# Up projection of an encoder layer: from the last row of the output projection on, the instructions of all five engines in a written order, with one split or sum of the next pair behind each chain

## Chip, cores, metric

One Trainium2 chip, one of its cores. The time is the device time of one execution in microseconds; of several runs the median is given. The engines of the core work in parallel, each through a queue of its own, and wait for each other by semaphores: TensorE (PE, matrix products; PEld is its weight load), VectorE (DVE), ScalarE (ACT), GpSimd (POOL) and SyncE (SP, which here issues transfers). PSUM is the memory of 8 banks into which TensorE writes; a bank holds 128 x 512 numbers in float32.

## What is computed

One layer of an encoder on 1024 tokens of width 1024: an input projection, attention in a window and a gated recurrence, a merge with an output projection, and a feed-forward part. The change concerns the seam between the last two.

```python
h = h + mix @ w_o[l]                       # output projection, residual
m = rms_norm(h, norm_mlp[l])               # a row's scale, times a gain
h = h + jnp.square(jax.nn.relu(m @ w_up[l])) @ w_down[l]
```

All inputs are float32. `w_up` is 1024 x 4096, `w_down` 4096 x 1024. The 1024 tokens are 8 row blocks of 128.

## The kernel before

**Products of float32.** An operand is split into a high part, rounded to the matmul type fp32r, and the rest: ScalarE casts (`wh`, `hi`), VectorE subtracts (`wl`, `lo`). A product is three matmuls, high by high, high by low, low by high.

**Output projection.** `wo_rows` (L889) makes half a row block by 24 matmuls and adds it into `hres` (L897). `norm_row` (L912) then issues the store of the row block, squares it on ScalarE (L919), takes 1/sqrt of the mean on GpSimd, and scales the row on VectorE (L921).

**Up projection.** It is one step of the Strassen-Winograd scheme, with seven products in place of eight. The left factor is a pair of column blocks of `w_up` (2 x 128 columns by two halves of the 1024 rows: a11, a12, a21, a22), the right one the normalised rows, transposed, in four quarters (b11, b12, b21, b22: half of the width by half of the tokens). There are NP = 16 pairs. For each, VectorE makes four sums of weights (`winograd`, L681 to L685):

```python
s1 = a21 + a22;  s2 = s1 - a11;  s3 = a11 - a21;  s4 = a12 - s2
```

and once for all pairs the rows give t1 to t4 (row loop, L948 to L951). The products are P1 = a11 b11, P2 = a12 b21, P3 = s4 b22, P4 = a22 t4, P5 = s1 t1, P6 = s2 t2, P7 = s3 t3, and each is a `chain` (L687) of 12 matmuls of 128 x 512: 4 steps of 128 rows, three matmuls each. Three banks take the seven: `pa` P1, then P1 + P2 (the block u11); `pb` P6, then P6 + P7, then P6 + P7 + P4; `pc` P3, then P3 + P5. ScalarE copies P1 and P3 out as `p1` and `p3` before the next chain goes into the same bank. VectorE and GpSimd then form the other blocks: u1 = pb + p1 + pc behind P5, u3 = pb + p1 - p3 + pc behind P7, u2 = pb + p1 behind P4. ScalarE applies ReLU and square (`relu2`, L982), and GpSimd forms four differences `S` of the blocks, which the down projection needs. All of them are stored to DRAM (`usp`), from where the down projection, which is also split like this, takes its operands.

**Weights.** `weights` (L974) splits one of a pair's seven left factors: a cast on ScalarE (L978) and a subtraction on VectorE (L979), 128 x 512 each. A pair's 1 MB of `w_up` comes by one transfer (`load_pair`, L1021), into one of two buffers. The weights' tiles `wh` and `wl` come from two pools in turn, four of each to a pool.

**Warm-up.** For the first three pairs (EARLY, L966) P1 and P2 are computed ahead (`first_products`, L989), as b11 and b21 are ready before t1 to t4 are. `to_variant` (L923) makes a piece of a right factor: TensorE transposes four 128 x 128 blocks into a bank `pt`, ScalarE casts them out (L929), VectorE subtracts (L930). Twenty such pieces remain after the last row; `psum_pools` gives this stretch the banks pa=2, a=4 (the transposes') and two for rows.

**What sets the order.** Up to here nothing is written by hand: a list scheduler decides, for each engine, in which order the instructions of this text stand, so chains, transposes and casts may be cut into each other. Only the down projection behind it has a written order (a block `manual_schedule`, L1289, in which each engine's queue keeps the order of the text).

**Main loop (L1045 to L1093).** In the text a pair's steps are: the load of the next pair, the four sums, all splits, P1 with the copy of p1, then P4 of the pair before with u2 and the last difference (`last_product`, L1035, held back by one pair), P3 with the copy of p3 (L1067), P2, P6 with u1's first sum (L1075), P5 with its second (L1077), P7, u3's three steps (L1080 on VectorE, L1081 on GpSimd, L1082 on VectorE), and the differences (L1087 to L1089). In the last pair VectorE takes the differences over from GpSimd. Behind the loop stand the operands of the down projection's first step (L1098 on) and its matmuls (`bk0`, L1115), which the casts in `split2` (L1152) follow.

Of the kernel before, what the change touches and what calls it, by code (L numbers as in the profile page):

```python
# [18 lines left out]
P = 128  # L19
# [29 lines left out]
def layer(ctx: ExitStack, tc: tile.TileContext, x, meta, w_in, w_na, w_hg, w_o, w_up, w_dn,  # L49
# [862 lines left out]
    def norm_row(i):  # L912
# [7 lines left out]
        rsqrt_mean(rs, ssq, D, tm)  # L920
        dve.scalar_tensor_tensor(hres[i], hres[i], rs, g2, op0=ALU.mult, op1=ALU.mult)  # L921

# [9 lines left out]
    for i in range(4):  # L932
        for hc in range(2):
            wo_rows(i, hc)
        norm_row(i)
    nT0 = u_tiles(0, "nT")
    nV = {"b11": [t[:, :4, :TH] for t in nT0], "b21": [t[:, 4:, :TH] for t in nT0]}

    nB = []
    for j in range(4):  # L940
        for hc in range(2):
            wo_rows(j + 4, hc)
        to_variant("a", hres[j][:, :TH], nV["b11"], j)
        to_variant("a", hres[j][:, TH:], nV["b21"], j)
        norm_row(j + 4)
        b11, b21, b12, b22 = (hres[i][:, q:q + TH] for i in (j, j + 4) for q in (0, TH))
        t2 = rowp.tile([P, TH], F32, tag="t2", name="t2", bufs=3)
        dve.tensor_tensor(b11, b12, b11, op=ALU.subtract)  # L948
        dve.tensor_tensor(t2, b22, b11, op=ALU.subtract)
        pool.tensor_tensor(b12, b22, b12, op=ALU.subtract)  # L950
        pool.tensor_tensor(b21, b21, t2, op=ALU.subtract)  # L951
        nB.append({"t1": b11, "b22": b22, "t3": b12, "t2": t2, "t4": b21})
# [33 lines left out]
    def first_tiles():  # L986
        return a_tile(upa, "p1", bufs=EARLY), a_tile(upa, "u11", bufs=EARLY)

    def first_products(w11, w12, between=lambda: None, tiles=None):  # L989
        p1, u11 = tiles or first_tiles()  # L990
        pa = up_bank("pa")
        chain(pa, w11, nV["b11"], True)
        act.copy(p1, pa)
        between()
        chain(pa, w12, nV["b21"], False)
        relu2(u11, pa)
        return p1, u11

    first_of, first_w = {}, {}

    def first_weights(m):
        raw = a_tile(upw, "sx", bufs=2, n=D).rearrange("p (k c) -> p k c", c=P)
        sp.dma_start(raw, w_up[:, 2 * m * P:(2 * m + 1) * P].rearrange("(k p) c -> p k c", p=P))
        first_w[m] = weights(raw[:, :4]), weights(raw[:, 4:])

    tiles = first_tiles()
    first_weights(0)

    for j in range(4):
        for v in nB[j]:  # L1010
            to_variant("a", nB[j][v], nV[v], j)
    rows_.close()
    hress.close()

    rawp = ups.enter_context(tc.tile_pool(name="rawp", bufs=1, side="right", reuse_waits="tile"))
    raws = {}

    def raw_tile():
        return rawp.tile([P, KC, 2 * P], F32, tag="raw", name="raw", bufs=2)

    def load_pair(m):  # L1021
        raws[m] = raw_tile()
        sp.dma_start(raws[m], w_up[:, 2 * m * P:(2 * m + 2) * P].rearrange("(k p) c -> p k c", p=P))

    load_pair(0)
    for m in range(EARLY):
        if m + 1 < EARLY:
            first_weights(m + 1)
        first_of[m] = first_products(*first_w[m], tiles=tiles if m == 0 else None)
        act.dma_start(usp[0][m][:, 0], first_of[m][1])  # L1030
    psum_pools(pa=2, pb=2, pc=2)
    upb = ups.enter_context(tc.tile_pool(name="upb", bufs=1, reuse_waits="tile"))
    w_pools.append(upb)

    def last_product(m, W, pb, p1, U, S):  # L1035
        chain(pb, W["a22"], nV["t4"], False)
        dve.tensor_tensor(U[2], pb, p1, op=ALU.add)
        relu2(U[2], U[2])
        last = m == NP - 1

# [5 lines left out]
    for m in range(NP):  # L1046
        if m + 1 < NP:
            load_pair(m + 1)
# [334 lines left out]
```

## Time and profile before

| | |
|---|---|
| median of 3 runs | 1548.38 us (1547.61 to 1549.24) |
| profiled execution, its own time | 1550.67 us |
| its span, first to last instruction | 1548.9 us |
| mean granted TensorE clock | 0.994 |
| PE busy, 0 to 860 us | 827.24 us |
| PE busy, 860 to 1245 us (last rows, up projection) | 380.75 of 385.00 us |
| PE busy, 1245 to 1549 us (down projection) | 295.16 of 304.00 us |

The views that the prediction quotes are these. The *page* gives the busy time of each engine. *Windows* are a table by stretch: start and end, length, busy time of each engine with its number of instructions, the granted clock, the share of DMA and its rate. *Waits* name the engine and line that waited, what released it, and the total, the number and the longest of these waits in us. *Timeline* rows have the start in us, the duration, engine, line, operation, output and inputs, shape, and in brackets the idle time ahead of the row and what ended it. Matmuls overlap, so their durations are longer than the distance from one to the next. `L691` to `L693` are the three matmuls of a chain's step, `L927` a group of four transposes.

### The profile page before, as it was taken

What the parts mean: (1) busy time and instruction counts of PE and PEld (TensorE: products, weight loads), DVE (VectorE), ACT (ScalarE), POOL (GpSimd) and SP (SyncE); (2) the same over time, 40 slices, a digit from 0 to 9 for tenths busy, and PEclk for the clock granted to TensorE, in tenths of its full rate; (3) what the DMA queues carried; (4) which work ended last, traced back from release to release, by engine and by line L of the source; (5) the groups of instructions that cost most, each with busy time, mean ns of one, the idle gap of its engine ahead of it and who ended that gap; (6) DMA issues with size and microseconds to landing.
All of it is one profiled execution on the core that took longest, in us unless ns stands there. A gap on an engine that the chain in (4) does not pass through costs nothing.

```text
span 1548.9 us, 23474 instructions
## 1 busy us (share of the span) xinstructions
PE 1503.1 (97%) x9188; PEld 1254.2 (81%) x9188; DVE 1010.7 (65%) x1588; ACT 657.7 (42%) x1172; POOL 407.2 (26%) x367
## 2 busy tenths in 40 slices
PE   5999999999999998999999999999999999999998
PEld 5788888887888887888888887888888788887886
DVE  6666666664976877666476368666666444879676
ACT  6231313124666666434123144555555433433444
POOL 4313121215224300011000122444444200237142
PEclk9999999999999999999999999999999999999999
DMA  5101011113123128434746124444444576563224
GB/s 181 43 28 56 28 56 29 55 29 120 57 72 119 55 68 271 137 123 151 260 161 229 55 83 140 149 157 152 155 151 144 170 273 235 190 231 105 100 82 150
DMA packets 142335, 195.61 MB, mean 126 GB/s; under 512 B 8064, under 2 KB 90112, under 8 KB 142224
## 3 DMA queue, kind: packets, MB, share of 16 engines
q1 hardware_dynamic: 133424, 172.61, 33.6%
q10 hardware_dynamic: 6624, 14.16, 2.4%
q0 software_dynamic: 2176, 7.34, 1.3%
q8 instruction: 72, 1.18, 0.3%
q14 instruction: 39, 0.32, 0.1%
HBM read 139.55 MB, written 54.53 MB: 125 GB/s over the span
## 4 chain that ended last, share of the span: by engine, by line
PE 85%; DVE 7%; issue 3%; ACT 2%; DMA 1%; POOL 1%; SPq 0%; POOLq 0%; ACTq 0%; DVEq 0%
PE mm L135 11%; PE mm L136 11%; PE mm L137 10%; PE mm L1106 4%; PE pa L1106 4%; PE pb L691 4%; PE pb L693 4%; PE pb L692 4%; PE pc L1106 4%; PE pb L1106 4%; PE pc L691 3%; PE pc L692 3%; PE pc L693 3%; PE pa L691 2%; PE pa L693 2%
## 5 line engine op out<-in xcount | busy, mean ns | idle before, releaser
L135 PE MATMUL mm<-aT,hi 128*128 128x512 f32 (+2 forms) x640 | 229.5, 359 | 2.1 <-DVE QX L563 1.5
L137 PE MATMUL mm<-aT,lo 128*128 128x512 f32 (+2 forms) x640 | 227.4, 355 | 0.0
L136 PE MATMUL mm<-aT,hi 128*128 128x512 f32 (+2 forms) x640 | 226.2, 353 | 0.0
L135 PEld LDWEIGHTS mm<-aT,hi 128*128 128x128 f32 x640 | 121.5, 190 | 16.4 <-issue 1.7
L97 DVE TENSOR_TENSOR dl<-ur,dh 128x1024 fp32r<-128x1024 f32 x55 | 76.8, 1396 | 88.4 <-ACT dh L96 88.3
L137 PEld LDWEIGHTS mm<-aT,lo 128*128 128x128 f32 x640 | 121.4, 190 | 13.2
L136 PEld LDWEIGHTS mm<-aT,hi 128*128 128x128 f32 x640 | 121.5, 190 | 12.5
L96 ACT CAST dh<-ur 128x1024 fp32r<-128x1024 f32 x55 | 57.9, 1053 | 161.3 <-issue 78.1
L125 ACT CAST hi<-raw 128x1024 fp32r<-128x1024 f32 x36 | 37.8, 1050 | 106.3 <-PE mm L136 75.5
L979 DVE TENSOR_TENSOR wl<-sx,wh 128x512 fp32r<-128x512 f32 x70 | 49.7, 719 | 32.3 <-ACT wh L978 32.3
L978 ACT CAST wh<-sx 128x512 fp32r<-128x512 f32 x70 | 42.7, 619 | 62.2 <-PE pc L692 27.3
L979 DVE TENSOR_TENSOR wl<-raw,wh 128x512 fp32r<-128x512 f32 x46 | 50.2, 1092 | 23.7 <-ACT wh L978 22.9
L1087 POOL TENSOR_TENSOR us<-u,uv 128x512 f32<-128x512 f32 x15 | 24.1, 1603 | 143.9 <-ACT uv L984 143.9
L1195 POOL TENSOR_TENSOR w<-w,tt 128x512 f32<-128x512 f32 x16 | 23.3, 1457 | 134.0 <-DVE tt L1194 106.0
L983 ACT ACTIVATE uv<-uv 128x512 f32<-128x512 f32 x48 | 30.4, 633 | 66.2 <-DVE uv L1082 49.9
L399 POOL TENSOR_TENSOR Y<-X,TN 128x512 f32<-128x512 f32 x20 | 33.8, 1690 | 88.2 <-DVE X L396 88.2
L126 DVE TENSOR_TENSOR lo<-raw,hi 128x1024 fp32r<-128x1024 f32 x34 | 45.5, 1338 | 16.1 <-ACT hi L125 15.3
L618 DVE CUSTOM_DVE_ANT_0 pr<-nsc,NB 128x432 f32<-128x432 f32 (+1 forms) x64 | 35.1, 558 | 27.0 <-PE nsc L613 26.8
L691 PE MATMUL pb<-nt,wh 128*128 128x512 f32 x128 | 51.0, 398 | 1.8 <-DVE uv L1075 1.8
L1106 PE MATMUL mm<-dl,dh 128*128 128x512 f32 x126 | 49.9, 396 | 2.1 <-DVE dl L97 2.1
L92 POOL TENSOR_SCALAR rtm<-ssq 128x1 f32<-128x1 f32 (+1 forms) x17 | 6.5, 385 | 172.2 <-ACT junk L919 157.6
L693 PE MATMUL pa<-nT,wl 128*128 128x512 f32 x128 | 50.3, 393 | 0.7 <-DVE wl L979 0.7
(381 smaller groups left out, 4422.5 us busy)
## 6 DMA issues: line engine op xcount, KB each, us to landing
raw<-in_w_in SPq DMA_DIRECT2D x56, 512.0 KB, 3.9
ur<-usp SPq DMA_DIRECT2D x55, 512.0 KB, 3.5
raw<-in_w_up SPq DMA_DIRECT2D x16, 1024.0 KB, 5.4
usp<-us SPq DMA_DIRECT2D x60, 256.0 KB, 2.0
sg<-gsp SPq DMA_DIRECT2D x16, 512.0 KB, 3.5
w<-in_w_dn SPq DMA_DIRECT2D x16, 512.0 KB, 4.5
usp<-uv SPq DMA_DIRECT2D x30, 256.0 KB, 2.3
gsp<-gv ACTq DMA_DIRECT2D x24, 256.0 KB, 2.7
```

The costliest lines, as they stand in the source:

```text
L96: act.copy(hi, src)
L97: dve.tensor_tensor(lo, src, hi.bitcast(F32), op=ALU.subtract)
L126: eng.tensor_tensor(lo[:, :kc], raw[:, :kc], hi[:, :kc].bitcast(F32), op=ALU.subtract)
L135: pe.matmul(ps, lh, rh, start=first, stop=False)
L136: pe.matmul(ps, lh, rl, start=False, stop=False)
L137: pe.matmul(ps, ll, rh, start=False, stop=last)
L691: pe.matmul(ps, lhs[0][:, c], rhs[0][:, k], start=first and k == 0, stop=False, skip_group_check=True)
L692: pe.matmul(ps, lhs[0][:, c], rhs[1][:, k], start=False, stop=False, skip_group_check=True)
L693: pe.matmul(ps, lhs[1][:, c], rhs[0][:, k], start=False, stop=k == 3, skip_group_check=True)
L978: act.copy(v(hi), src)
L979: dve.tensor_tensor(v(lo), src, v(hi).bitcast(F32), op=ALU.subtract)
L1106: pe.matmul(ps, a[n == 2][:, q, j * P:(j + 1) * P], b[n == 1][:, q], start=first and n == 0, stop=last and n == 2, skip_group_check=True)
```

## The change

The list scheduler is set aside from the last row block (row 7) of the output projection to the last product of the up projection. This stretch now stands in a `manual_schedule` block over all five engines: each engine carries out its instructions in the order of the text. To write that order, the steps are cut into functions, `product_1` to `product_7` named by product, and the main loop calls them so that behind each chain one split of the *next* pair's weights follows (`next_weights`); the four sums of the next pair (`pair_sums`) stand between u3 and P4 of the pair before. A pair's weights are loaded two pairs ahead.

```diff
+    def row_scale(i):
...
         act.dma_start(hsp[i], hres[i])
         act.activation(junk, hres[i], AF.Square, accum_out=ssq)
         rsqrt_mean(rs, ssq, D, tm)
+        return rs
+    def scale_row(i, rs):
         dve.scalar_tensor_tensor(hres[i], hres[i], rs, g2, op0=ALU.mult, op1=ALU.mult)
+    def row_sums(j):
...
+    for i in range(4, 8):
         for hc in range(2):
+            wo_rows(i, hc)
+        if i < 6:
+            for j in (2 * i - 8, 2 * i - 7):
+                to_variant("a", hres[j][:, :TH], nV["b11"], j)
+                to_variant("a", hres[j][:, TH:], nV["b21"], j)
+        if i < 7:
+            scale_row(i, row_scale(i))
+            if i > 4:
+                nB += [row_sums(j) for j in range(len(nB), i - 3)]
...
+    def next_weights(m, *vs):
+        if m + 1 == NP:
+            n = len(step0)
+            if n < 4:
+                step0.append(weights(step0_raw[0][:, n * TH:(n + 1) * TH]))
+            return
+        q = pairs[m + 1]
+        for v in vs:
+            if not (q.early and v in ("a11", "a12")):
+                q.W[v] = weights(q.A[v])
+    def product_1(q, w):
...
+        chain(q.pa, w, nV["b11"], True)
+        act.copy(q.p1, q.pa)
+    def product_2(q, w):
+        chain(q.pa, w, nV["b21"], False)
+        relu2(q.u11, q.pa)
+        (act if q.early or q.last else sp).dma_start(usp[0][q.m][:, 0], q.u11)
+    def product_3(q):
+        q.pc, q.p3 = up_bank("pc"), a_tile(upb, "p3")
+        chain(q.pc, q.W["s4"], nV["b22"], True)
+        act.copy(q.p3, q.pc)
+    def product_6(q):
...
+        chain(q.pb, q.W["s2"], nV["t2"], True)
+        dve.tensor_tensor(q.u1, q.pb, q.p1, op=ALU.add)
+    def product_5(q):
+        chain(q.pc, q.W["s1"], nV["t1"], False)
+        dve.tensor_tensor(q.u1, q.u1, q.pc, op=ALU.add)
+        relu2(q.u1, q.u1)
+    def block_out(q, v, a, b, op, dst):
+        q.S[v] = a_tile(upb, "us", bufs=4)
+        (dve if q.last else pool).tensor_tensor(q.S[v], a, b, op=op)
+        (pool if q.last else sp).dma_start(dst, q.S[v])
+    def product_7(q):
+        q.u3 = a_tile(upb, "uv", bufs=6)
+        chain(q.pb, q.W["s3"], nV["t3"], False)
+        dve.tensor_tensor(q.u3, q.pb, q.p1, op=ALU.add)
+        pool.tensor_tensor(q.u3, q.u3, q.p3, op=ALU.subtract)
+        block_out(q, 2, q.u11, q.u1, ALU.subtract, usp[2][q.m][:, 1])
+    def finish_u3(q):
+        dve.tensor_tensor(q.u3, q.u3, q.pc, op=ALU.add)
+        relu2(q.u3, q.u3)
+        (act if q.last else sp).dma_start(usp[2][q.m][:, 0], q.u3)
+        block_out(q, 0, q.u1, q.u3, ALU.add, usp[1][q.m][:, 1])
+        block_out(q, 1, q.S[0], q.u11, ALU.subtract, usp[1][q.m][:, 0])
+    def product_4(q):
...
+        chain(q.pb, q.W["a22"], nV["t4"], False)
+        dve.tensor_tensor(u2, q.pb, q.p1, op=ALU.add)
+        relu2(u2, u2)
...
+    first_load(0)
+    first_load(1)
+    first_weights(0)
+    first_weights(1)
+    first_load(2)
+    with tc.manual_schedule(engines={e.engine for e in (pe, act, dve, pool, sp)}):
+        rs7 = row_scale(7)
...
+        product_1(pairs[0], first_w[0][0])
+        transposes(0, 4)
+        scale_row(7, rs7)
+        product_2(pairs[0], first_w[0][1])
+        transposes(4, 6)
+        nB.append(row_sums(3))
+        transposes(6, 9)
+        product_1(pairs[1], first_w[1][0])
+        first_weights(2)
+        transposes(9, 14)
+        product_2(pairs[1], first_w[1][1])
+        transposes(14, 20)
...
+        load_pair(0)
+        load_pair(1)
+        product_1(pairs[2], first_w[2][0])
+        pair_sums(pairs[0])
+        next_weights(-1, "s4", "s2")
+        product_2(pairs[2], first_w[2][1])
+        psum_pools(pa=2, pb=2, pc=2)
...
+        next_weights(-1, "s1", "s3", "a22")
+        for m, q in enumerate(pairs):
+            if m + 2 <= NP:
+                load_pair(m + 2)
+            if not q.early:
+                product_1(q, q.W["a11"])
+            if m:
+                finish_u3(pairs[m - 1])
+            if m + 1 < NP:
+                pair_sums(pairs[m + 1])
+            if m:
+                product_4(pairs[m - 1])
+            next_weights(m, "a11", "s4")
+            product_3(q)
+            next_weights(m, "a12")
+            if not q.early:
+                product_2(q, q.W["a12"])
+            next_weights(m, "s2")
+            product_6(q)
+            next_weights(m, "s1")
+            product_5(q)
+            next_weights(m, "s3")
+            product_7(q)
+            next_weights(m, "a22")
+        finish_u3(pairs[-1])
+        product_4(pairs[-1])
```

`transposes(n0, n1)` calls `to_variant` for the pieces n0 to n1 - 1 of the twenty, five to a row block: t1, b22, t3, t2, t4. The seventeenth `load_pair` fetches the operands of the down projection's first step. In the rows below, numbers behind a name tell buffers apart.

ScalarE's queue at the passage from the warm-up to the loop. `pa` is the bank of pair 2's P1 and P2, the `sx` tiles hold two sums each (before, 9454 holds s1 and s2 of pair 0, 9455 s3 and s4, 9557 and 9558 those of pair 1; after, 9427, 9428 and 9485 in the same way), `pc` is the bank of pair 0's P3. Before:

```order
L978 CAST wh_9464<-sx_9454 128x512
L993 COPY p1_9407<-pa_9409 128x512
L978 CAST wh_9460<-sx_9455 128x512
L978 CAST wh_9468<-sx_9454 128x512
L978 CAST wh_9472<-sx_9455 128x512
L978 CAST wh_9476<-raw_9325 128x512
L983 ACTIVATE u11_9408<-pa_9409 128x512
L984 ACTIVATE u11_9408<-u11_9408 128x512
L1030 DMA usp0_2_8515<-u11_9408 128x512
L978 CAST wh_9567<-sx_9557 128x512
L978 CAST wh_9575<-sx_9558 128x512
L1067 COPY p3_9482<-pc_9481 128x512
```

After, the same place:

```order
L1051 COPY p1_9411<-pa_9413 128x512
L988 CAST wh_9433<-sx_9428 128x512
L988 CAST wh_9437<-sx_9427 128x512
L993 ACTIVATE u11_9412<-pa_9413 128x512
L994 ACTIVATE u11_9412<-u11_9412 128x512
L1056 DMA usp0_2_8515<-u11_9412 128x512
L988 CAST wh_9470<-sx_9427 128x512
L988 CAST wh_9474<-sx_9428 128x512
L988 CAST wh_9478<-raw_9407 128x512
L988 CAST wh_9490<-sx_9485 128x512
L1061 COPY p3_9495<-pc_9494 128x512
```

Three casts of pair 0 (s1, s3, a22) now stand behind ReLU, square and store of pair 2's u11 instead of ahead of them, and the cast ahead of the copy of p3 is now that of pair 1's s4 (wh_9490), the last of its four sums; before, those of its s2 and s3 stood there.

TensorE at the end of pair 0's P7 (`pb` its bank, nt30 and nt31 the parts of t3, nt40 and nt41 those of t4, nT10 and nT11 those of b22). Before, with `pc_9584` the bank of pair 1's P3:

```order
L691 MATMUL pb_9480<-nt30_9153,wh_9472 128x512
L692 MATMUL pb_9480<-nt31_9154,wh_9472 128x512
L693 MATMUL pb_9480<-nt30_9153,wl_9473 128x512
L691 MATMUL pc_9584<-nT10_9146,wh_9563 128x512
L692 MATMUL pc_9584<-nT11_9147,wh_9563 128x512
L693 MATMUL pc_9584<-nT10_9146,wl_9564 128x512
L691 MATMUL pc_9584<-nT10_9146,wh_9563 128x512
L691 MATMUL pb_9480<-nt40_9155,wh_9476 128x512
```

After:

```order
L691 MATMUL pb_9513<-nt30_9139,wh_9474 128x512
L692 MATMUL pb_9513<-nt31_9140,wh_9474 128x512
L693 MATMUL pb_9513<-nt30_9139,wl_9475 128x512
L691 MATMUL pb_9513<-nt40_9141,wh_9478 128x512
L692 MATMUL pb_9513<-nt41_9142,wh_9478 128x512
L693 MATMUL pb_9513<-nt40_9141,wl_9479 128x512
```

The four matmuls of pair 1's P3 that stood between P7 and P4 are gone from there: P4 follows P7 at once in the same bank.

TensorE where the second group of transposes begins (`pa` is pair 0's bank, `pt` the bank of a transpose). Before, seven pieces stand ahead of these rows, and more are cut into the chain of P2:

```order
L693 MATMUL pa_9337<-nT00_8818,wl_9177 128x512
L691 MATMUL pa_9337<-nT00_8818,wh_9176 128x512
L927 MATMUL pt_9229<-ident_80,hres5_8496 128x128 x4
L692 MATMUL pa_9337<-nT01_8819,wh_9176 128x512
L927 MATMUL pt_9236<-ident_80,t2_8975 128x128 x4
L693 MATMUL pa_9337<-nT00_8818,wl_9177 128x512
L927 MATMUL pt_9243<-ident_80,hres1_8495 128x128 x4
L927 MATMUL pt_9250<-ident_80,hres2_8489 128x128 x4
```

After, behind the whole chain of P2 and ahead of the next pair's P1:

```order
L693 MATMUL pa_9188<-nT00_8818,wl_9163 128x512
L940 MATMUL pt_9246<-ident_80,hres0_8493 128x128 x4
L940 MATMUL pt_9253<-ident_80,hres1_8495 128x128 x4
L940 MATMUL pt_9265<-ident_80,hres5_8496 128x128 x4
L940 MATMUL pt_9272<-ident_80,hres5_8496 128x128 x4
L940 MATMUL pt_9279<-ident_80,t2_9003 128x128 x4
L691 MATMUL pa_9288<-nT00_8818,wh_9166 128x512
```

Five pieces now stand in a row, for four banks; before, at most two stood together here, with matmuls of a chain around them.

157 lines of the change are left out of this document (47 added, 110 removed).

## Prediction

> **What bounds the kernel now.** I read the page first, then the busy time by stretch, then TensorE's waits in the part that the change rewrites (875 to 1245 us).
>
> ```profile
> span 1548.9 us, 23474 instructions
> PE 1503.1 (97%) x9188; PEld 1254.2 (81%) x9188; DVE 1010.7 (65%) x1588; ACT 657.7 (42%) x1172; POOL 407.2 (26%) x367
> ```
> ```profile
> core 0: us, PE busy (x) PEld busy (x) DVE busy (x) ACT busy (x) POOL busy (x), PEclk, DMA share, GB/s
> 911.00:931.00 20.00, 19.06 (x125) 15.85 (x124) 17.63 (x27) 15.69 (x30) 3.33 (x4) 1.00 0.43 146
> 961.00:969.00 8.00, 6.15 (x20) 4.36 (x19) 5.07 (x9) 2.50 (x4) 1.60 (x2) 0.79 0.57 194
> 1000.00:1200.00 200.00, 200.00 (x885) 165.58 (x884) 126.39 (x169) 104.65 (x181) 82.72 (x55) 1.00 0.44 153
> ```
> ```profile
> PE pb L691 <- DVE uv L1075: 1.8, 1, 1.8
> PE mm L1106 <- ACT dh L96: 0.7, 1, 0.7
> PE pa L693 <- DVE wl L979: 0.7, 1, 0.7
> PE mm L1106 <- DVE dl L97: 0.4, 1, 0.4
> PE pb L691 <- ACT wh L978: 0.3, 1, 0.3
> PE pa L691 <- ACT nT L929: 0.2, 1, 0.2
> ```
> TensorE bounds the kernel. From 1000 to 1200 us, ten pairs of the up projection, it never waits, at the full clock: a written order has nothing to win there. All its waits in the whole part come to 4.1 us, and the 1.1 us of L1106 belong to the down projection behind it. At 911 to 931 VectorE (17.63 of 20 us) and ScalarE (15.69) are nearly full too. So the change must win in the warm-up, where three engines are loaded at once, and can lose anywhere.
>
> ```profile
> 923.20 0.60 PE L927 MATMUL pt<-ident,hres 128*128 128x128 f32 x4
> 923.56 0.48 PE L692 MATMUL pa<-nT,wh 128*128 128x512 f32 x1
> 923.87 0.60 PE L927 MATMUL pt<-ident,hres 128*128 128x128 f32 x4
> ...
> 963.27 0.50 PE L691 MATMUL pb<-nt,wh 128*128 128x512 f32 x1 [1.85 <-DVE uv L1075]
> ...
> 1076.68 0.39 PE L691 MATMUL pa<-nT,wh 128*128 128x512 f32 x1
> 1079.40 0.39 PE L691 MATMUL pb<-nt,wh 128*128 128x512 f32 x1
> ```
> A chain of 12 matmuls takes 2.72 us (1079.40 - 1076.68), 0.227 each. A matmul lasts 0.39, so a chain's end E is 0.16 us later than the moment at which the next chain could start. Four transposes and one matmul take 0.67 (923.87 - 923.20), that is 4 x 0.11 + 0.23: mixing them is free. The first matmul after a wait lasts 0.50, 0.11 longer: each wait costs its length and 0.1.
>
> **What goes.** The waits of 0.24, 0.70, 0.33 and 1.85 us with 0.1 to 0.2 behind each, some 0.6 at 911 to 913 us where the first chain starts haltingly, and 0.3 where chains are cut into each other: about 5.0. The stretch 961 to 969 also shows the clock at 0.79: (1 - 0.79) x 8 = 1.7 us lost after the 1.85 us wait. Together **-6.7 us**, if all of it goes.
>
> **What comes, with these prices.** ScalarE:
> ```profile
> 934.12 0.60 ACT L983 ACTIVATE u<-pa 128x512 f32<-128x512 f32 x1 [3.78 <-PE pa L693]
> 934.75 0.63 ACT L984 ACTIVATE u<-u 128x512 f32<-128x512 f32 x1
> 935.41 0.33 ACTq L1030 DMA_DIRECT2D usp<-u  x1
> 935.78 0.62 ACT L978 CAST wh<-sx 128x512 fp32r<-128x512 f32 x1 [0.40 <-ACT u L984]
> 936.31 0.58 ACT L993 COPY p<-pa 128x512 f32<-128x512 f32 x1
> 936.78 1.66 ACT L978 CAST wh<-sx 128x512 fp32r<-128x512 f32 x3
> ```
> ReLU, square and the issue of the store hold ScalarE 1.66 us (935.78 - 934.12). Casts follow each other every 0.52 ((1.66 - 0.62) / 2); a copy takes 0.58. VectorE and GpSimd:
> ```profile
> 939.86 0.68 DVE L682 TENSOR_TENSOR sx<-raw 128x512 f32<-128x512 f32 x1
> ...
> 941.78 0.69 DVE L685 TENSOR_TENSOR sx<-raw,sx 128x512 f32<-128x512 f32 x1
> ...
> 957.32 1.67 DVE L682 TENSOR_TENSOR sx<-raw 128x512 f32<-128x512 f32 x1
> 959.02 1.67 DVE L683 TENSOR_TENSOR sx<-sx,raw 128x512 f32<-128x512 f32 x1
> ```
> ```profile
> 958.51 1.62 POOL L1041 TENSOR_TENSOR us<-uv,us 128x512 f32<-128x512 f32 x1
> ```
> Alone, the four sums of a pair take 2.6 us (939.86 to 942.47) and a split's subtraction 0.6 to 0.69; beside a GpSimd operation a sum takes 1.67. Handing over between engines costs 0.03 (935.41 after 934.75 + 0.63).
>
> *First chain.* `product_1` of pair 0 now follows the last output row at once, and its bank is one that VectorE still reads for that row's sum: 0.16 + 0.03 + 0.69 + 0.03 + 0.1 = **1.0**. Before, eight transposes stood there.
>
> *Transposes in groups.* There are four `pt` banks. In the groups 4..8, 9..13 and 14..19 the fifth transpose of a group waits until the first one's bank is read. In the first and third group its cast stands behind ReLU, square and store of the chain just ended: E + 0.03 + 1.66 + 0.59 + 0.03 + 0.69 + 0.03 = E + 3.0, against E - 0.16 + 4 x 0.44 = E + 1.6; in the second it stands behind a copy and two casts, and VectorE's two subtractions give E + 3.0 too. Three waits of 1.4 and 0.1: **4.5**. Nothing hides them; only four more banks would.
>
> *Pair 2's second chain* waits for the copy of the first out of the same bank: 0.16 + 0.03 + 0.59 + 0.03 + 0.1 = **0.9**.
>
> *The p3 copy in pairs 0, 1 and 2.* `product_5` overwrites the bank that `product_3` filled, so it waits for the copy p3, and on ScalarE that copy now stands behind the cast of the next pair's s4, which needs that pair's four sums. Pair 0, from the end E of pair 2's second chain: ReLU to store 1.7, three casts to the end of the last 1.66, its subtraction 0.63, the four sums 2.61, cast and copy 0.03 + 0.52 + 0.58 + 0.03: E + 7.75. TensorE has only products 3 and 6 to do: E - 0.16 + 5.44 = E + 5.28. The wait is 2.5. Pair 1, from the start A of the sum u3 behind product 7: 0.72, GpSimd's subtraction after VectorE's a22 split 1.7, u3's second sum 0.7, then four sums that alternate with GpSimd's block differences, until 8.5 (two pass beside 1.67 each, as in the rows), the sum u2 until 9.1, ReLU and square until 10.33, cast and copy: A + 11.46; TensorE has products 4, 3 and 6, so it is there at A + 0.72 + 0.11 + 8.16 = A + 9.0. The wait is 2.5; in pair 2 two casts stand ahead, 3.0. With 0.1 each: **8.3**. Bounds: with sums of 2.6 us all through, pairs 1 and 2 pay nothing and it is 2.6; with all four at 1.67 it is 10. I take 8.3, since both engines' rows at 957 to 960 alternate just so.
>
> *Product 7 straight before product 4* in pairs 0 and 1, in one bank: between them VectorE must read it, after the s3 split. That sum starts 3.2 us behind product 5's end (0.72 sum, 0.66 + 0.54 ReLU and square, 0.65 cast, 0.6 subtraction), ends at 3.9, and product 4 could have started at 2.56: 1.4 + 0.1, twice: **3.0**. Before, four matmuls of the next pair stood between.
>
> *From pair 3 on* products 1 and 2 fill these gaps. There the chain through ScalarE, VectorE and GpSimd from one u3 to the next comes to 19.1 to 19.2 us by the same rows, against 7 x 2.72 = 19.04 on TensorE: 12 pairs x 0 to 0.4; I take 0.04 each, **0.5**, the lower end, as the order before held 200.00 of 200.
>
> *The end.*
> ```profile
> 1233.55 0.69 DVE L1088 TENSOR_TENSOR us<-uv 128x512 f32<-128x512 f32 x1 [1.36 <-ACT uv L984]
> 1234.16 0.68 DVE L1037 TENSOR_TENSOR uv<-pb,p 128x512 f32<-128x512 f32 x1
> 1234.76 0.68 DVE L1089 TENSOR_TENSOR us<-us,u 128x512 f32<-128x512 f32 x1
> ```
> In the last pair the sum u2 (L1037) stands ahead of the second difference; the new order puts it behind (0.72), and GpSimd's subtraction of p3 behind S2 (0.4). The down projection's first operands are cast behind it: **1.1** more on the wait of 0.7.
>
> *The clock.*
> ```profile
> 585.00:592.00 7.00, 4.65 (x20) 3.71 (x20) 6.46 (x10) 5.17 (x11) 0.00 (x0) 0.76 0.80 291
> 360.00:367.00 7.00, 5.51 (x38) 5.04 (x38) 3.89 (x8) 3.67 (x10) 6.25 (x7) 1.00 0.43 144
> ```
> ```profile
> PE ppt L633 <- DVE PT L645: 2.4, 1, 2.4
> PE mm L135 <- DVE QX L563: 1.5, 1, 1.5
> ```
> The waits of 2.4 and 1.85 us were followed by a lower granted clock (0.76 of 7 us, 0.79 of 8 us), one of 1.5 us was not. Three of the new waits are 2.5 to 3.0: 3 x 1.7, less 0.9 for work that catches up meanwhile, **4.2**; bounds 0 and 6.8 (a fourth, at the end). [...]
>
> **Sum.** 1.0 + 4.5 + 0.9 + 8.3 + 3.0 + 0.5 + 1.1 + 4.2 = 23.5; 23.5 - 6.7 = **+16.8 us**. The profiled execution took 1550.67 us (span 1548.9 and 1.8 around it), 2.3 over the median; with the change about 1567.5 there, and 1548.4 + 16.8 = **1565 us** as the median, 1.1% slower.
>
> **Rivals.**
> 1. *The loop of pairs 3 to 15 becomes the bound.* At 0.4 a pair instead of 0.04 the time is 1565 + 4 = 1569, and to 1575 with a low clock at the end. For it: 19.2 against 19.04. Against: ten pairs without a wait before.
> 2. *The clock holds.* Without the 4.2, and with one p3 wait gone because the sums meet GpSimd less, 1558.
> 3. *Not slower: a cast that waits doesn't hold the copies behind it.* The place is ScalarE's queue; if p3's copy starts when its chain ends, up to 8.3 us after u3, the 8.3, the 4.5, 0.8 of the 3.0 and the 4.2 go, 17.8: 23.5 - 17.8 - 6.7 = -1.0, 1547. Against it: in the rows above the cast at 935.78 begins when the store ahead of it is issued, 0.40 after the square, and every waiting row there holds the ones behind it. [...]
>
> **How the numbers follow.** Forecast 0.70, rival 1 0.14, rival 2 0.08, rival 3 0.08. A measurement of this kernel tells 0.2%, 3 us, from no change. Rival 3 lies within it, and half of it below if the loop gains too: faster 0.04, same 0.04, slower 0.92. The range takes in both rivals of the slower side, 1556 to 1575; below it lies rival 3.
>
> **What would show it.** In the profile after: TensorE waiting three times for the copy of p3 (2.5 to 3.0 us each), twice for u3's first sum (1.4), three times in a transpose for VectorE (1.4), some 1.8 for the down projection's first cast, and a clock under 1 in two or three places between 945 and 1000 us. From pair 3 on, TensorE without waits over 0.4. It would be wrong if those p3 waits are missing, or if a wait of 2.5 us leaves the clock at 1.

## The result, and the profile after

| | before | changed |
|---|---|---|
| median | 1548.81 us (4 runs) | 1566.32 us (4 runs, 1564.57 to 1567.28) |
| ratio | | 1.0113, 95% interval 1.0095 to 1.013 |
| span of the profiled execution | 1548.9 us | 1564.9 us |
| start of the last matmul of the last row to that of the first matmul on operands from `split2` (L1106; L1169 in the changed kernel) | 327.90 us | 341.05 us |
| from there to the last matmul | 303.25 us | 304.83 us |

Forecast were 1565 us and +16.8; measured are 1566.3 and +17.5. Ratios here and below are those of the mean times, without one execution of the kernel before (3668 us) and one of run e8 (3851 us), each more than twice as long as all others.

The matmuls of the down projection's first step (`bk0`) lie partly among the last product's; its second step starts with the first operands that `split2` casts, and there the stretch of the last row but one ends and that of the last row begins. Of the 327.90 us before, 0.88 are two transposed pieces (8 x 0.11) that the changed kernel does ahead of this stretch (88 transposes lie in it before, 80 after), so the stretch grew by 341.05 - 327.02 = 14.0 us, and what lies behind it by 1.6.

The waits of TensorE in the changed kernel from 905 to 1256 us, all that the view lists (who waited, for whom; us in total, times, longest):

```profile
PE pc L691 <- ACT p L1061: 7.3, 3, 2.6
PE pt L940 <- DVE nt L943: 4.0, 3, 1.4
PE pb L691 <- DVE uv L1081: 2.4, 2, 1.2
PE mm L1169 <- ACT dh L96: 1.6, 1, 1.6
PE pa L691 <- DVE hres L897: 0.9, 1, 0.9
PE pa L691 <- ACT p L1051: 0.7, 1, 0.7
PE mm L1169 <- DVE dl L97: 0.4, 1, 0.4
```

Each line but the last, which stood at 0.4 before too, is one term of the forecast, with its count: product 5 behind the copy of p3 in three pairs, the fifth transpose of three groups, product 4 behind u3's first sum in two pairs, the down projection's first cast, the first chain's bank, pair 2's second chain. The wait for L1075 (1.8 us before) is gone. A wait counts from the end of the last matmul; since matmuls overlap by 0.16 us (one lasts 0.39 and the next starts 0.227 after it) and the first after a wait lasts 0.11 longer (0.50), it costs 0.27 more than its row says (0.2 in a transpose).

The timeline of TensorE at product 5 of pairs 0, 1 and 2, and the windows of the loop behind the third wait and from there on (the clock is the column PEclk):

```profile
952.13 0.50 PE L691 MATMUL pc<-nt,wh 128*128 128x512 f32 x1 [2.53 <-ACT p L1061]
...
969.70 0.50 PE L691 MATMUL pc<-nt,wh 128*128 128x512 f32 x1 [2.12 <-ACT p L1061]
...
987.76 0.50 PE L691 MATMUL pc<-nt,wh 128*128 128x512 f32 x1 [2.61 <-ACT p L1061]
```
```profile
988.34:991.75 3.41, 3.41 (x10) 2.67 (x9) 2.81 (x5) 0.93 (x2) 0.00 (x0) 0.50 0.21 82
...
1025.00:1200.00 175.00, 175.00 (x774) 144.91 (x773) 124.68 (x147) 90.67 (x161) 67.26 (x46) 1.00 0.47 155
```

The third wait is followed by half the clock (0.50 from 988.34 to 991.75 us), the other two are not (1.00 from 950.79 to 954.20 and from 970 to 980 us), though the first is only 0.08 us shorter; and from 1025 to 1200 us the new order runs as the old one did, without a wait.

| term | forecast, us | in this profile, us |
|---|---|---|
| waits and low clock that go | -6.7 | -7.0 |
| first chain's bank | 1.0 | 1.1 |
| transposes in groups | 4.5 | 4.0 + 3 x 0.2 = 4.6 |
| pair 2's second chain | 0.9 | 0.7 + 0.27 = 1.0 |
| copy of p3, pairs 0 to 2 | 8.3 | 7.3 + 3 x 0.27 = 8.1 |
| product 7, then product 4 | 3.0 | 2.4 + 2 x 0.27 = 2.9 |
| pairs 3 to 15 | 0.5 | 0 |
| the end | 1.1 | 1.6 - 0.75 = 0.9 |
| low clock | 4.2 | 2 x 3.41 x 0.5 = 3.4 |
| sum | 16.8 | 15.0 |

(-7.0 is what TensorE lost from 905 to 1230 us in the profile of before: each distance from one matmul's start to the next, less the 0.2267 of a dense passage, or 0.11 in a transpose.) The span grew by 16.0; of the 1.0 that is left, 0.4 lies ahead of the stretch, and 0.6 is not accounted for.

### The profile page after: what moved, and what is told of

Read it like the earlier page. It is cut to its first block, busy times and chain, and to the rows that moved or that the text cites. A ratio compares the mean times of both kernels' runs of the same rounds, so it can differ in the third digit from the quotient of the medians.

```text
span 1564.9 us, 23484 instructions
## 1 busy us (share of the span) xinstructions
PE 1506.5 (96%) x9188; PEld 1255.0 (80%) x9188; DVE 1027.7 (66%) x1588; ACT 655.2 (42%) x1172; POOL 405.4 (26%) x367
## 4 chain that ended last, share of the span: by engine, by line
PE 84%; DVE 7%; ACT 3%; issue 3%; DMA 2%; POOL 1%; SPq 0%; ACTq 0%; POOLq 0%; DVEq 0%
PE mm L135 11%; PE mm L136 10%; PE mm L137 10%; PE mm L1169 4%; PE pa L1169 4%; PE pb L691 4%; PE pc L1169 4%; PE pb L692 4%; PE pb L693 4%; PE pb L1169 4%; PE pc L691 3%; PE pc L693 3%; PE pc L692 3%; PE pa L691 2%; PE pa L693 2%
## 5 line engine op out<-in xcount | busy, mean ns | idle before, releaser
L97 DVE TENSOR_TENSOR dl<-ur,dh 128x1024 fp32r<-128x1024 f32 x55 | 77.3, 1406 | 90.0 <-ACT dh L96 89.9
L135 PEld LDWEIGHTS mm<-aT,hi 128*128 128x128 f32 x640 | 121.3, 190 | 17.1 <-issue 1.7
L993 ACT ACTIVATE uv<-uv 128x512 f32<-128x512 f32 x48 | 30.4, 632 | 119.0 <-DVE uv L1096 66.4
L989 DVE TENSOR_TENSOR wl<-sx,wh 128x512 fp32r<-128x512 f32 x70 | 48.2, 696 | 41.6 <-ACT wh L988 41.6
L1082 POOL TENSOR_TENSOR uv<-uv,p 128x512 f32<-128x512 f32 x16 | 25.8, 1611 | 155.3 <-ACT wh L988 106.3
L989 DVE TENSOR_TENSOR wl<-raw,wh 128x512 fp32r<-128x512 f32 x46 | 42.2, 918 | 29.2 <-ACT wh L988 29.2
L1169 PE MATMUL mm<-dl,dh 128*128 128x512 f32 x126 | 50.1, 397 | 2.1 <-DVE dl L97 2.1
L691 PE MATMUL pa<-nT,wh 128*128 128x512 f32 x128 | 50.4, 394 | 1.5 <-DVE hres L897 0.9
L1169 PE MATMUL mm<-dh 128*128 128x512 f32 x126 | 49.0, 391 | 1.6 <-ACT dh L96 1.6
L135 PE MATMUL mm<-wh,mT 128*128 128x512 f32 x128 | 50.2, 392 | 0.0
```

What stands on the lines that cost most here:

```text
L97: dve.tensor_tensor(lo, src, hi.bitcast(F32), op=ALU.subtract)
L135: pe.matmul(ps, lh, rh, start=first, stop=False)
L691: pe.matmul(ps, lhs[0][:, c], rhs[0][:, k], start=first and k == 0, stop=False, skip_group_check=True)
L989: dve.tensor_tensor(v(lo), src, v(hi).bitcast(F32), op=ALU.subtract)
L1169: pe.matmul(ps, a[n == 2][:, q, j * P:(j + 1) * P], b[n == 1][:, q], start=first and n == 0, stop=last and n == 2, skip_group_check=True)
```

## The experiments

Two theories stood against each other for the largest term. **Q**, which the prediction's words say: the copy of p3 is late because of its place in ScalarE's queue, and product 4 because it stands next to product 7; cure the place and the wait goes. **S**: in pairs 0 to 2 TensorE has five chains, 13.6 us, and the string of sums, splits, ReLUs and differences on VectorE, ScalarE and GpSimd from one pair to the next is longer; cure one place and the next one waits.

Code ahead of the written order, the same in the changed kernel and in all kernels below, took more or less time from run to run: the last row's last matmul started at 911.58 us in one profile of the changed kernel and at 907.60 in another, and the medians of the two series are 3.3 us apart (e9). So medians alone can't tell 3 us here, and beside them stands the **stretch** of the table above, 341.05 us in the changed kernel, from one profile of each kernel; in the changed kernel it repeats to 0.1 us (run e9).

**e1: copy of p3 first.**

```diff
+            if q.early:
+                product_3(q)
             next_weights(m, "a11", "s4")
-            product_3(q)
+            if not q.early:
+                product_3(q)
```

> The changed kernel with one edit: in pairs 0, 1 and 2 the copy of p3 stands on ScalarE ahead of the casts of the next pair's a11 and s4, not behind them. Theory Q (the prediction's step: the copy waits only because of its place in ScalarE's queue): the three waits of product 5 (7.3 us, with their restarts 7.6) go, and with them the half clock behind the third (1.6): 1566.3 - 9.2 = 1557. Theory S (the string of VectorE, ScalarE and GpSimd work for the next pair is longer than the five chains that TensorE has in pairs 0 to 2, so the next thing in the string is late instead): product 7 or product 4 wait in its place, the period of a pair from one product 3 to the next stays at 17 to 18 us, and 0 to 2.5 us go: 1563.8 to 1566.3.

Median 1560.28 us (ratio 1.0082, 1.0064 to 1.01), stretch 337.98: 3.1 shorter, of which 1.7 is the half clock behind the third wait (3.41 x 0.5), now missing. TensorE's waits from 940 us on:

```profile
PE pc L691 <- ACT p L1061: 3.2, 2, 1.6
PE pb L691 <- DVE uv L1081: 2.6, 2, 1.3
PE pb L691 <- DVE uv L1066: 2.1, 2, 1.3
...
```

The wait in pair 0 left product 5 (the copy now starts at 944.10, half a microsecond behind its chain), and half of it came back at product 7, which waits for u1's first sum (L1066) on VectorE; the sums and splits that this stands behind did not move. There waits of 2.53 and 1.22 us became 1.25 and 1.34: 1.2 less. In pairs 1 and 2 1.6 us stay at product 5, and there the edit did not bring the copy to its chain's end. In pair 1 the chain ends at 960.35 us, and the copy starts 3.7 us later, behind ReLU and square of the u2 of pair 0, whose sum (L1096) stands behind the four sums:

```profile
962.86 0.63 ACT L993 ACTIVATE uv<-uv 128x512 f32<-128x512 f32 x1 [4.50 <-DVE uv L1096]
963.52 0.63 ACT L994 ACTIVATE uv<-uv 128x512 f32<-128x512 f32 x1
964.06 0.57 ACT L1061 COPY p<-pc 128x512 f32<-128x512 f32 x1
```

So theory Q is tested in full in pair 0 alone. Over all three pairs 7.9 us in 6 waits stand against 9.7 in 5: 1.8 less, 1.4 with the restarts, much nearer to theory S (0 to 2.5) than to Q. From one product 3 to the next pass 16.8 and 17.1 us in place of 18.0 and 17.6. The median lies between the two forecasts; in the profiled run 3.3 us of that are a shorter way to the stretch.

**e2: product 3 of the next pair between product 7 and product 4.**

```diff
-            if m:
+            if m and not q.early:
                 product_4(pairs[m - 1])
             next_weights(m, "a11", "s4")
             product_3(q)
+            if m and q.early:
+                product_4(pairs[m - 1])
```

> The changed kernel with one edit: for pairs 0 and 1 product 4 stands behind the next pair's product 3, not straight behind product 7. Theory Q (the two waits of product 4 come from two chains standing next to each other in one bank): they go, 2 x (1.2 + 0.3) = 3.0 us: 1563.3. Theory S (the string for the next pair sets the period): product 5 or product 7 of the next pair wait longer by the same amount, 0 to 0.7 us gained or lost: 1565.6 to 1567.

Median 1566.30 us (1.0113, 1.0097 to 1.0128), stretch 343.04. The waits from 940 to 1000 us:

```profile
PE pc L691 <- ACT p L1061: 6.5, 3, 2.5
PE pb L691 <- DVE uv L1066: 4.0, 2, 2.3
```

Product 4's waits (2.4) are gone, and product 7 of pairs 1 and 2 waits 4.0 in their place: 0.8 us more in all. Theory S again. The rest of the 2.0 us by which the stretch is longer is a second passage of low clock (0.52 in the window from 947.72 to 951.13 us).

**e3: ReLU, square and store behind the transposes.** `second_group` is the group of the pieces 4 to 8; the splits of pair 2's first weights move behind their group too.

```diff
+    def product_2(q, w, between=lambda: None):
         chain(q.pa, w, nV["b21"], False)
+        between()
         relu2(q.u11, q.pa)
...
+        product_2(pairs[0], first_w[0][1], second_group)
         product_1(pairs[1], first_w[1][0])
-        first_weights(2)
         transposes(9, 14)
-        product_2(pairs[1], first_w[1][1])
-        transposes(14, 20)
+        first_weights(2)
+        product_2(pairs[1], first_w[1][1], lambda: transposes(14, 20))
```

> The changed kernel with one edit: ReLU, square and store of u11 (pairs 0 and 1) stand behind the five or six transposes that follow the chain, and the two splits of pair 2's first weights behind the five that follow product 1 of pair 1; all groups keep their size. Theory of the prediction (the fifth transpose waits because its bank's cast stands behind ReLU, square and store, 1.66 us, or behind a copy and two casts): the waits of 1.4 us fall to E + 0.59 + 0.69 + 0.09 + 0.28 against E + 1.6, about 0.1 to 0.3 each, 3.5 to 4 us gone: 1562.5. Rival (four banks for five pieces, or VectorE's pace of 0.6 to 0.69 a piece, set it, whatever ScalarE does first): the waits stay at 1 us or more each, 1565 to 1566.

Median 1560.08 us (1.0072, 1.0055 to 1.0089), stretch 337.39, 3.7 shorter. Of the waits up to 945 us two lines are left:

```profile
PE pa L691 <- DVE hres L897: 0.9, 1, 0.9
PE pa L691 <- ACT p L1051: 0.7, 1, 0.7
```

The line of L940 (4.0) is gone from the view, with the same groups of five or six in four banks (waits of 0.1 us are left, too short for it). What stood ahead of the first cast was the cause, as forecast, not the number of banks.

**e4: pair 0's splits ahead of pair 2's second chain.**

```diff
...
         next_weights(-1, "s4", "s2")
+        w_pools.insert(0, upb)
+        next_weights(-1, "s1", "s3", "a22")
         product_2(pairs[2], first_w[2][1])
         psum_pools(pa=2, pb=2, pc=2)
...
-        next_weights(-1, "s1", "s3", "a22")
```

> The changed kernel with one edit: the splits of pair 0's s1, s3 and a22 stand ahead of pair 2's second chain, so on ScalarE ahead of ReLU, square and store of its u11 (as in the kernel before), not behind them. VectorE idles 2.66 us at 943.85 to 946.51 for these casts before the four sums of pair 1. If the first of the three waits of product 5 comes from this delay (the sums of pair 1 start 2.7 us earlier), it falls from 2.6 to 0.3 or less, 2.4 us gone; the waits of pairs 1 and 2 stay, as their strings start at u3 of the pair before: 1563.9. If VectorE's lead carries on, those shrink too: 1559 to 1562. If the copy is late for another reason: 1566.

Median 1562.29 us (1.009, 1.0075 to 1.0105). The timeline of VectorE in the changed kernel shows what this is about, splits of pair 0 (L989), then the sums of pair 1:

```profile
946.51 1.29 DVE L989 TENSOR_TENSOR wl<-sx,wh 128x512 fp32r<-128x512 f32 x2 [2.66 <-ACT wh L988]
947.72 0.69 DVE L989 TENSOR_TENSOR wl<-raw,wh 128x512 fp32r<-128x512 f32 x1
948.33 0.69 DVE L682 TENSOR_TENSOR sx<-raw 128x512 f32<-128x512 f32 x1
...
950.26 0.68 DVE L685 TENSOR_TENSOR sx<-raw,sx 128x512 f32<-128x512 f32 x1
```

VectorE stood still for 2.66 us, since the casts were queued behind the ReLU of a chain that had not ended. With the casts ahead of it the wait of product 5 in pair 0 is gone, those of pairs 1 and 2 are still 4.7 us in two, and the stretch is 339.93: 2.8 us less wait, with one passage of low clock more (1.7; the clock is 0.50 from 966.02 and from 986.50 us, for 3.41 us each). The copy itself kept its place behind the cast of s4. So the head of the string in pair 0 is the place of these casts.

**e5: no differences in pairs 0 to 2.** The kernel leaves out the four differences there and stores a block in the place of each; so it computes something else, and only its times are of use.

```diff
     def block_out(q, v, a, b, op, dst):
+        if q.early:
+            (pool if q.last else sp).dma_start(dst, a)
+            q.S[v] = a
+            return
```

> The changed kernel without the four block differences of pairs 0, 1 and 2 (GpSimd's L1075; a block is stored in their place), so that GpSimd has only the subtraction of p3 there. In the changed kernel's profile the sums of pair 2 take 1.17, 0.69, 1.78 and 1.78 us beside GpSimd. If this sharing is what makes the string of pairs 1 and 2 longer than the five chains (theory S with GpSimd as its cause), the sums fall to 0.69 each and the waits of product 5 in pairs 1 and 2 (2.3 and 2.8 us) fall below 0.4, while that of pair 0 (2.6, before which GpSimd does nothing) and those of product 4 (1.2 each) stay. If the string is long by its order alone, they stay over 1.5 us. Span some 5 to 7 us below the 1564.9 of the changed kernel, or within 2.

One run, 1560.66 us, stretch 335.87. Product 5 waits once, 2.5 us, in pair 0; in pairs 1 and 2 no longer. The four sums of pair 2 (L682 to L685), first in the changed kernel, then here:

```profile
961.44 1.17 DVE L682 TENSOR_TENSOR sx<-raw 128x512 f32<-128x512 f32 x1
962.64 0.69 DVE L683 TENSOR_TENSOR sx<-sx,raw 128x512 f32<-128x512 f32 x1
963.25 1.78 DVE L684 TENSOR_TENSOR sx<-raw 128x512 f32<-128x512 f32 x1
964.95 1.78 DVE L685 TENSOR_TENSOR sx<-raw,sx 128x512 f32<-128x512 f32 x1
```
```profile
962.13 0.69 DVE L682 TENSOR_TENSOR sx<-raw 128x512 f32<-128x512 f32 x1
...
964.06 0.68 DVE L685 TENSOR_TENSOR sx<-raw,sx 128x512 f32<-128x512 f32 x1
```

5.29 us beside GpSimd (961.44 to 966.73), 2.61 without it. With these 2.7 us a pair the waits of 2.1 and 2.6 us in pairs 1 and 2 are gone, and here too the copy kept its place behind the cast of s4.

**e6: pairs 0 to 2 in another order.** To e4 comes:

```diff
         for m, q in enumerate(pairs):
+            if q.early:
+                load_pair(m + 2)
+                if m == 0:
+                    product_3(q)
+                    pair_sums(pairs[1])
+                else:
+                    product_3(q)
+                    finish_u3(pairs[m - 1])
+                    product_4(pairs[m - 1])
+                product_6(q)
+                product_5(q)
+                next_weights(m, "s4", "s2") if m < 2 else next_weights(m, "a11", "s4")
+                product_7(q)
+                next_weights(m, "s1", "s3") if m < 2 else next_weights(m, "a12", "s2", "s1", "s3", "a22")
+                if m < 2:
+                    pair_sums(pairs[m + 2])
+                    next_weights(m, "a22")
+                continue
```

> The changed kernel with pairs 0 to 2 written in another order, all else the same: pair 0's splits ahead of ReLU and square of pair 2's u11 (as in the run before this one that moved them); the four sums of pair m + 2 a pair earlier, straight behind u3's first sum of pair m; product 4 behind the next pair's product 3; u1 and its ReLU ahead of the next casts. Theory S (the string must start earlier, no single place in a queue is to blame): the 11.2 us of waits in pairs 0 to 2 (three of product 5, two of product 4, with restarts) fall below 2.5 and the low clock behind the third goes: 1566.3 - 8.7 - 1.6 = 1556. Against it (VectorE has 13.4 us of work in a pair of 13.6, so no order can hide it): at least 6 us of waits stay, 1561 or more.

Median 1554.77 us (1.0047, 1.0034 to 1.006), stretch 331.84, 9.2 shorter. The waits of the loop that are left, with the clock at 1.00 from 945 to 1200 us:

```profile
PE pc L691 <- ACT p L1061: 0.6, 1, 0.6
PE pb L691 <- DVE uv L1066: 0.5, 1, 0.5
...
PE pa L693 <- DVE wl L989: 0.3, 1, 0.3
PE pc L693 <- DVE wl L989: 0.2, 1, 0.2
```

GpSimd and VectorE do the same work as in the changed kernel, and it fits: the string was not too long for 13.6 us, it was begun too late.

**e7: the last pair.** u3 - p3 by `dve` in place of `pool`; in `product_4` of the last pair u2, its ReLU and store stand ahead of the differences (`more_out` holds two of them; that of block 2 moves behind u3's store).

```diff
-        pool.tensor_tensor(q.u3, q.u3, q.p3, op=ALU.subtract)
+        (dve if q.last else pool).tensor_tensor(q.u3, q.u3, q.p3, op=ALU.subtract)
...
         (act if q.last else sp).dma_start(usp[0][q.m][:, 1], u2)
+        if q.last:
+            more_out(q)
```

> The changed kernel with the last pair alone in another order: u3 minus p3 on VectorE (0.69 us) in place of GpSimd (1.62 us), and u2's sum, ReLU and square ahead of the three differences. By the prediction's step (u2 stands behind S1 and GpSimd's subtraction, and the down projection's first casts behind u2's ReLU) the casts start 2.0 to 2.5 us earlier and the wait of 1.6 us (1.78 with its restart) in front of the down projection goes; the one of 0.4 us behind it stays: 1.9 us less, and 1.4 more where the low clock had followed: 1563 to 1564.4. If the casts wait for something else, a store or the last matmuls: within 0.5 of 1566.3.

Median 1562.65 us (1.0092, 1.0079 to 1.0105), stretch 339.18, 1.9 shorter; behind it 302.99 in place of 304.83. The wait of 1.6 us is gone, 0.3 for L97 is left, and no low clock follows.

**e8: all of it.** e3, e6 and e7 together; two pieces ahead of the first chain, pair 2's first chain ahead of pair 1's second, in pair 3 u2 ahead of the sums and p3's copy ahead of the casts.

```diff
+        transposes(0, 2)
         product_1(pairs[0], first_w[0][0])
-        transposes(0, 4)
+        transposes(2, 4)
+        first_w[2] = [weights(first_raw[2][:, :4])]
...
         product_1(pairs[1], first_w[1][0])
-        first_weights(2)
+        first_w[2].append(weights(first_raw[2][:, 4:]))
         transposes(9, 14)
+        product_1(pairs[2], first_w[2][0])
+        transposes(14, 20)
         product_2(pairs[1], first_w[1][1])
-        transposes(14, 20)
```

> All of it together: ReLU behind the transposes; two transposed pieces ahead of the first chain; pair 2's P1 ahead of pair 1's P2 with its weights split earlier, so that no two chains of one bank stand next to each other in the warm-up; pairs 0 to 2 in the order of the run e6; in pair 3 u2 ahead of the sums and p3's copy ahead of the next casts; the last pair as in e7. If the waits are independent terms as the prediction summed them, what is left of 24.4 us lost in the stretch is about 0.8 in the transposes, 2 in pairs 0 to 3 and 0.6 at the end, with no low clock, some 5 us against the 8.7 of the kernel before: 1548.5 - 3 = 1545.5, faster than both. If each cure brings a new wait, 1548 to 1556.

Median 1547.09 us against 1548.12 (ratio 0.9992, 0.9983 to 1.0001): not to be told from the kernel before. The stretch is 324.40. The two pieces ahead of the first chain are two of the same twenty (80 transposes in the stretch, as in the changed kernel), so it compares with 327.02 of before: 2.6 us less, of which 1.7 was low clock in that profile (0.50 from 963.92 to 967.33 us). It ran again:

> The kernel of the run e8 once more, to tell 0.1% from 0.2% against the kernel before. The profiles give 324.4 us against 327.9 from the last row's last matmul to the down projection, but 1.6 of that is low clock in the profiled run of the kernel before, which need not follow in each of its runs. Median 1 to 3 us below that of the kernel before on the same chip; if the gain is given back behind the stretch, within 0.5 us of it.

Median 1544.81 against 1548.84 us, ratio 0.9981, 0.9972 to 0.999, stretch 324.52. All that is left of TensorE's waits:

```profile
PE pt L940 <- DVE nt L943: 0.8, 1, 0.8
PE pb L691 <- DVE uv L1067: 0.3, 1, 0.3
PE mm L1206 <- DVE dl L97: 0.3, 1, 0.3
PE pc L693 <- DVE wl L989: 0.3, 1, 0.3
PE pa L693 <- DVE wl L989: 0.2, 1, 0.2
```

Faster than the kernel before by 0.1 to 0.3% in this comparison; the first one allows no gain at all. All the cures together bring back what the written order lost, and whether they bring more is not settled.

**e9: the changed kernel once more, for the clock.**

> The changed kernel once more, unaltered, for the clock. Theory W (the clock is set for stretches of 3.41 us on a fixed grid that the kernel doesn't move: a stretch in which TensorE idles for about 1.9 us or more is followed by one at half clock, whatever the length of the single wait): the waits are those of the first profile within 0.1 us (2.6, 2.3 and 2.6 for product 5, 1.2 twice for product 4, 1.6 at the end), but the low clock may stand behind others of them; all starts and ends of low clock lie multiples of 3.41 us apart, and each is led by a stretch with 1.9 us or more of idle time, while none with less leads one. Rival (the length of the wait, or what has gathered before it, decides): the low clock stands behind the third wait and the one at the end again, not behind the first two. Time 1566 in both.

Median 1563.03 us (1.0093, 1.0078 to 1.0107), stretch 341.02 against 341.05; the same seven lines of waits, within 0.1 us. The low clock stands behind the third wait (0.53 in the window from 984.46 to 987.87 us), but this time not at the end. The windows at the end, in the first profile and in this one (3.41 us with the wait of 1.6 in them, then the next 3.41):

```profile
1251.17:1254.58 3.41, 1.59 (x6) 1.01 (x7) 2.60 (x5) 3.41 (x6) 0.54 (x1) 1.00 0.79 279
1254.58:1257.99 3.41, 3.41 (x10) 2.64 (x9) 2.27 (x3) 0.50 (x1) 0.00 (x0) 0.50 0.83 232
```
```profile
1247.48:1250.89 3.41, 1.90 (x7) 1.29 (x8) 2.82 (x4) 3.41 (x6) 0.54 (x1) 1.00 0.79 275
1250.89:1254.30 3.41, 3.41 (x17) 2.79 (x16) 1.95 (x3) 0.18 (x1) 0.00 (x0) 1.00 0.80 255
```

The same wait, a little more or less of it in one window: in the first TensorE is busy 1.59 us and half the clock follows, in the second 1.90 and it does not. The two low stretches of the first profile start at 988.32 and 1254.56 us, 266.24 us apart, which is 78 times 3.4133. In the same profile a low stretch starts at 612.85 us, 110 times 3.4133 ahead of the first of these; in the kernel before two start at 588.45 and 963.92 us, 110 times apart, and in e4 three at 587.14, 966.02 and 986.50 us, 111 and 6 times apart. So far this is theory W. Its rival, the length of the wait, falls: the wait of 1.85 us before was followed by the low clock, that of 2.53 us in the changed kernel was not, and that of 1.6 us at the end was in one profile of the changed kernel and not in the other.

## Why the prediction was right, and where not

**What goes.** -6.7 against -7.0: none of the four waits that it counted is left (those of L1106, ahead of the down projection's second step, were not among them).

**First chain, transposes, pair 2's second chain.** Sizes held. For the transposes the cause did too: e3 took what stood ahead of the casts away, and 3.7 of 4.6 us went with it. "Nothing hides them; only four more banks would" was wrong, as e3 has the same four banks. For the other two the cause is read from the rows of the waits, and both are gone in e8, which puts other work in these places.

**The copy of p3.** Size right (8.3 against 8.1), but the words named the last link of the string as the cause, and rival 3 priced it by them: if p3's copy started when its chain ends, the 8.3 would go. In pair 0 of e1 it does start then, and 1.2 of 2.5 us go. The other way round, in e4 (pair 0) and e5 (pairs 1 and 2) the copy keeps its place in the queue and the waits go. The working itself had gone along the string (ReLU to store, three casts, the four sums; then u3, the sums beside GpSimd, u2), and that is why the number came out near. What each part of it costs the runs show apart: the casts behind a ReLU that waits, 2.7 us (e4), and sums beside GpSimd, 2.7 us in each of the two later pairs (e5). The prediction's lower bound for this term, 2.6 us with all sums at their own pace, is what e5 shows (one wait of 2.5).

Part of the size is luck. The waits were forecast at 8.0 us and came to 7.3, and a restart costs 0.27, not 0.1, which nearly makes up for it. The working gives the four sums 5.4 us (from 3.1 to 8.5), though two at 1.67 and two at 0.69 make 4.7; it does not say where the rest comes from. The trace has 5.29, as one of the other two sums is longer too: 1.17, 0.69, 1.78, 1.78. The 0.03 us for a step between engines was read from a row within ScalarE's own queue; the changed kernel shows it between engines (VectorE's L1087 ends at 961.52, ScalarE's L993 starts at 961.55).

**Product 7 straight before product 4.** Size right, cause wrong in the same way: "before, four matmuls of the next pair stood between" is true, but with the twelve of product 3 between them (e2) the string is no shorter and product 7 waits instead.

**Pairs 3 to 15.** 0.5 forecast, 0 measured; the rival of a loop that becomes the bound (19.2 us of string against 19.04) fell with the row of 175.00 us.

**The end.** 1.1 against 0.9, by the cause given (e7).

**The clock.** 4.2 against 3.4, near by luck: the rule behind it failed. Of three waits of 2.1 to 2.6 us, each longer than the 1.85 us after which the clock had fallen before, one was followed by a low clock; the other low clock came at the end of the loop, behind waits of 1.6 and 0.4 us. The prediction forecast two or three places between 945 and 1000 us, and there is one. It also named as a sign of being wrong a wait of 2.5 us that leaves the clock at 1: the first wait of product 5 did that. Rival 2 (the clock holds, and one wait of product 5 goes) fell: all three waits are there, though the clock held behind two of them. The 3.4 are two low stretches of 3.41 us at 0.50.

**The total.** +16.8 forecast, +17.5 between the medians, +16.0 between the profiles. A second series of the same kernel (e9) has a median of 1563.03 us in place of 1566.32, +14.2 over the kernel before, so that the first came within 1.3 us of the forecast is partly luck. In the two profiled runs, 5.7 us apart, 4.0 us lie ahead of the stretch and 1.6 behind it, where e9 has no low clock; for the other runs there is no profile.

## What to carry to other kernels

A wait names the last link of a string; before its place in a queue is blamed, move that one instruction and see whether the wait goes or only moves on (in pair 0 of e1 a wait of 2.5 us was worth 1.2). A written order needs, for each stage, enough matmul time for what runs beside it: one split behind each chain holds here with seven chains a pair (no wait from 1025 to 1200 us), not with five (9.7 us of waits in pairs 0 to 2), unless the work of the next pair starts a pair earlier (1.6 us in the loop of e6). And an instruction that waits for a chain not yet ended, such as ReLU, belongs behind the casts that others need (2.8 us less wait in e4).

## What the hardware showed that was not expected

In these profiles the granted clock fell to 0.50 for stretches of 3.41 us, and the starts given under e9 lie, within each profile, whole multiples of 3.4133 us apart. The starts at 963.92 us before and at 988.32 us in the changed kernel tell where this grid lies in the two profiles. Take as idle time each distance from one matmul's start to the next, less 0.227 us (0.11 in a transpose, 0.427 at half clock). Between 900 and 1300 us three stretches on the grid were followed by one at half clock: that from 960.50 us before, in which TensorE idled 2.12 us, and those from 984.91 and 1251.15 us in the changed kernel, with 2.88 and 2.26. In all others there it idled less, and none of them was: at most 1.99 us in the changed kernel (from 967.84 us, behind the second wait of product 5) and 1.70 before (from 1236.98 us). (The 1.9 in the expectation of e9 counts the longer first matmul after a wait as work.) What the hardware counts is not shown: the busy time of the windows, which takes in the overlap ahead of a wait, does not tell the two kinds apart (1.59 of 3.41 us led to it at the end of the changed kernel, 1.55 from 967.84 us on did not). The first wait of product 5, 2.53 us, was cut by a border into two parts of 1.3 and 1.5 us of idle time, and cost no clock (the first column behind the length is the busy time of TensorE; the clock is the third from the end):

```profile
947.38:950.79 3.41, 2.22 (x10) 1.50 (x8) 3.38 (x6) 0.14 (x1) 0.00 (x0) 1.00 0.29 78
950.79:954.20 3.41, 2.07 (x9) 1.73 (x10) 2.42 (x5) 2.14 (x4) 0.00 (x0) 1.00 0.65 229
```

So in these traces a wait of 1.85 us cost 1.7 us more (before), and one of 2.53 us nothing, as the grid happened to lie.
